# Differential attention: scoring both maps of a head together, the second passes on 64 rows each

## The chip, the core and the metric

The kernel runs on one core of a Trainium2 chip. The metric is the device time of one execution in microseconds (us). The engines are named as the profile names them: PE is TensorE (matrix products), PEld is its weight loads, DVE is VectorE, ACT is ScalarE, POOL is GpSimd, and SP issues most of the transfers.

## The reference, cut to what matters

One layer: a half feed-forward step, a mixer of two attention branches side by side, and a second half feed-forward step. The change lies in branch B of the mixer, differential attention with 4 heads. Each head has two softmax maps over the same 1024 positions; the second, scaled by a learned number, is taken from the first, and the difference multiplies the values:

```
s1 = einsum('bhqd,bhkd->bhqk', qi1, k1) * scale + bias        # d = 64
s2 = einsum('bhqd,bhkd->bhqk', qi2, k2) * scale + bias
p = softmax(where(allowed, s1, NEG)) - lam * softmax(where(allowed, s2, NEG))
out = einsum('bhqk,bhkd->bhqd', p, v)
```

The mask lets a row see whole chunks of 64 up to its own, so a block of 128 query rows, number qb from 0 to 7, needs the first (qb + 1) x 128 keys.

## The kernel before, in words

Products of nearly full float32 accuracy are made from operands in a reduced format (fp32r). Each number x is kept as a high part xH, which is x rounded, and a low part xL, the rest. A product is then xH times yH, plus xL times yH, plus xH times yL, three passes of PE that add up in one bank of PSUM.

In the mixer a *unit* is a pair of stick-breaking heads (units 0 to 3) or one differential head (units 4 to 7). For each unit, QJob and KJob project the queries and the keys. A projection gives 128 rows: 64 for map 0 and 64 for map 1. The depth of a score is only 64, while PE takes 128 rows, and the kernel uses the spare half for the low parts:

- QJob (L1064) writes the tile q. For map i, 64 rows hold qH and the other 64 rows hold qL. For map 0 qH is on the lower half (rows 0 to 63, `lo`), for map 1 on the upper half (`hi`).
- KJob (L1081) writes kd, with kH on both halves, and kl, with kL on both halves. ACT and DVE fill one half, and POOL copies it to the other (L1097 for kd, L1098 for kl).

One score tile z is then two passes of 128 rows, in the function qk (L1164): q against kd (L1169) gives qH kH + qL kH, and q against kl (L1170) adds qH kL and, as a by-product, the tiny qL kL. A z tile is 128 query rows by up to 512 keys (`pieces` cuts the keys at 512); there are three z buffers in PSUM, shared with a few other small tiles.

da_weights (L1269) makes the weights of two query blocks, 2j and 2j + 1. For each block and each map in turn, every piece is scored, DVE subtracts the distance bias from z, writes the result to ex and takes the row maximum (L1280), then DVE negates the maximum (L1286), ACT takes the exponential and the row sum (L1288) and DVE the reciprocal (L1290). At the end of the block DVE scales map 1 (L1295) and subtracts it from map 0 (L1296). The function av transposes these weights (L1188, L1189, tiles trp), and da_out multiplies them by the values (L1306, L1308, tile pav).

Attention alone would leave PE waiting. `fill(n)` therefore puts projection passes of the next unit and of the gates (pps, L1044 to L1048) between the steps of the attention, in proportion. The order on each engine is then fixed when the program is built: a planner takes the recorded instructions and sets each engine's queue, in which instructions run strictly one after the other. Differential units run from about 1041 us to 1340 us of the profile.

Of the kernel before, what the change touches and what calls it, by code (L numbers as in the profile page):

```python
# [12 lines left out]
F32 = mybir.dt.float32  # L13
# [7 lines left out]
P = 128  # L21
D = 1024
S = 1024
NK = D // P
NT = S // P
HALF = 512
# [16 lines left out]
SCALE = 1.0 / math.sqrt(HD)  # L43
# [3 lines left out]
def build(ctx, tc, A, out):  # L47
# [945 lines left out]
    pending = ffn("wg1", "wu1", "wd1", start0, pending0, steps1, lambda c: 0 if c < 3 else 5 if c < 9 else 4 if c == 9 else 0, steps1b, 0, lambda t: A["x"][t * P:(t + 1) * P, :], lambda t: h_dram[0][t])  # L993

    pending = mixer(locals())

    ffn("wg2", "wu2", "wd2", start_half, pending, steps2, lambda c: 2 if c > 1 else 0, no_steps, 2, lambda t: h_dram[1][t],
# [4 lines left out]
def mixer(e):  # L1002
# [5 lines left out]
    V, ACT, PE, POOL, SP = nc.vector, nc.scalar, nc.tensor, nc.gpsimd, nc.sync  # L1008
# [8 lines left out]
    with tc.tile_pool(name="mixa", bufs=1, side="left", reuse_waits="tile") as pa, \  # L1017
            tc.tile_pool(name="mix_ps", bufs=2, space=PSUM, reuse_waits="tile") as psum, stack:
        lo, hi = slice(0, HD), slice(HD, P)


        class Job:


            def __init__(self, srcs):
                self.srcs = srcs
                self.order = (0, 1)
                self.w = None
                self.it = None
# [22 lines left out]
            def columns(self, half):  # L1052

                ps = psum.tile([P, HALF], F32, name="pps", tag="gu")
                H, L = self.w[0]
                yield from self.product(ps, [((H[:, k * P:(k + 1) * P], L[:, k * P:(k + 1) * P]), U[k, half]) for k in range(NK)])
                return ps

            def run(self):
                for half in self.order:  # L1060
                    yield from self.half(half)
                    yield

        class QJob(Job):  # L1064
# [6 lines left out]
            def half(self, half):  # L1071
                if half == 0:
                    self.out = pa.tile([P, 2, S], F32R, name="q", tag="q", bufs=2)
                q = self.out
                sl = slice(half * HALF, (half + 1) * HALF)
                ps = yield from self.columns(half)
                for i, (rh, rl) in enumerate(((lo, hi), (hi, lo))):
                    ACT.mul(q[rh, i, sl], ps[rh], self.scale)
                    V.scalar_tensor_tensor(q[rl, i, sl], ps[rh], self.scale, q[rh, i, sl].bitcast(F32), ALU.mult, ALU.subtract)

        class KJob(Job):  # L1081


            def __init__(self, block):
                super().__init__([A["win"][block]])

            def half(self, half):
                if half == 0:
                    self.out = (pa.tile([P, 2, S], F32R, name="kd", tag="kd", bufs=2),
                                pa.tile([P, 2, S], F32R, name="kl", tag="kl", bufs=2))  # L1090
                kd, kl = self.out
                sl = slice(half * HALF, (half + 1) * HALF)
                ps = yield from self.columns(half)
                for i, (rh, rl) in enumerate(((lo, hi), (hi, lo))):
                    ACT.copy(kd[rh, i, sl], ps[rh])
                    V.tensor_sub(kl[rh, i, sl], ps[rh], kd[rh, i, sl].bitcast(F32))
                    POOL.tensor_copy(kd[rl, i, sl], kd[rh, i, sl])  # L1097
                    POOL.tensor_copy(kl[rl, i, sl], kl[rh, i, sl])  # L1098

        class GateJob(Job):  # L1100
            def __init__(self, gi, c):
# [40 lines left out]
        last_pe = [None]  # L1142
# [3 lines left out]
        def advance(n):  # L1146

            if n > 0 and keep[0]:
                with tc.issue_after(last_pe[0].ins):
                    advance_(n)  # L1150
            else:
                advance_(n)
# [11 lines left out]
        def qk(q, k, i, qb, c0, c1):  # L1164

            z = psum.tile([P, HALF], F32, name="z", tag="z", bufs=3)[:, :c1 - c0]
            qs = slice(qb * P, (qb + 1) * P)
            kd, kl = k
            PE.matmul(z, q[:, i, qs], kd[:, i, c0:c1], start=True, stop=False)  # L1169
            last_pe[0] = PE.matmul(z, q[:, i, qs], kl[:, i, c0:c1], start=False, stop=True)  # L1170
            return z

        def pieces(qb):
            L = (qb + 1) * P
            return L, [(c0, min(c0 + HALF, L)) for c0 in range(0, L, HALF)]
# [59 lines left out]
        def sb_weights(hp, par, j, q, k, fill):  # L1235
            ws = []
            for qb in (2 * j, 2 * j + 1):
                L, cuts = pieces(qb)
                be = mp.tile([P, S], F32, name="be", tag="wa", bufs=4)
                f = mp.tile([P, S], F32, name="f", tag="wb", bufs=2)  # L1240
                for c0, c1 in cuts:
                    z = qk(q, k, par, qb, c0, c1)
                    if c1 == L:
                        PE.matmul(z[:, c1 - P - c0:], identb, mask_sb, start=False, stop=True, skip_group_check=True)
                    ACT.activation(be[:, c0:c1], z, AF.Sigmoid)
                    last_act[0] = ACT.activation(f[:, c0:c1], z, AF.Sigmoid, scale=-1.0)
                    fill(1)
                yield
                fr = f[:, :L][:, ::-1]
                V.tensor_tensor_scan(fr, fr, fr, 1.0, ALU.mult, ALU.bypass)  # L1250
                V.tensor_mul(be[:, :L - 1], be[:, :L - 1], f[:, 1:L])
                ws.append(be)
            yield ws
# [15 lines left out]
        def da_weights(h, j, q, k, fill):  # L1269
            slope = 2.0 ** (-8.0 * (h + 1) / DA_HEADS)  # L1270
            ws = []
            for qb in (2 * j, 2 * j + 1):
                L, cuts = pieces(qb)
                es, rs = [], []
                for m in range(2):
                    ex = mp.tile([P, S], F32, name="ex", tag="wa" if m == 0 else "wb", bufs=4 if m == 0 else 2)
                    mx = mp.tile([P, 2], F32, name="mx", tag="mx", bufs=4)
                    for i, (c0, c1) in enumerate(cuts):
                        z = qk(q, k, m, qb, c0, c1)
                        V.tensor_tensor_reduce(out=ex[:, c0:c1], in0=z, in1=dist[:, S - L + c0:S - L + c1], op0=ALU.subtract,  # L1280
                                               op1=ALU.max, scale=1.0, scalar=NEG, accum_out=mx[:, i:i + 1])
                        fill(1)
                    nm = mp.tile([P, 1], F32, name="nm", tag="nm", bufs=4)
                    if len(cuts) == 2:
                        V.tensor_max(mx[:, 0:1], mx[:, 0:1], mx[:, 1:2])
                    V.tensor_scalar_mul(nm, mx[:, 0:1], -slope)  # L1286
                    sm = mp.tile([P, 1], F32, name="sm", tag="sm", bufs=4)
                    ACT.activation(ex[:, :L], ex[:, :L], AF.Exp, bias=nm, scale=slope, accum_out=sm)  # L1288
                    r = mp.tile([P, 1], F32, name="r", tag="r", bufs=4)
                    V.reciprocal(r, sm)  # L1290
                    es.append(ex)
                    rs.append(r)
                r2 = mp.tile([P, 1], F32, name="r2", tag="r2", bufs=4)
                V.tensor_mul(r2, rs[1], lam)
                V.tensor_scalar_mul(es[1][:, :L], es[1][:, :L], r2)  # L1295
                V.scalar_tensor_tensor(es[0][:, :L], es[0][:, :L], rs[0], es[1][:, :L], ALU.mult, ALU.subtract)  # L1296
                ws.append(es[0])
            return ws
# [30 lines left out]

        def qk_jobs(u):  # L1330
            if u < 4:
                return QJob(u, SCALE), KJob(4 + u)
            h = u - 4
            slope = 2.0 ** (-8.0 * (h + 1) / DA_HEADS)
            return QJob(12 + h, SCALE / slope), KJob(16 + h)


        cur = qk_jobs(0)
        vjob = VJob(0, 0)
        first = [cur[0], cur[1], vjob]  # L1340
# [13 lines left out]
        mp = stack.enter_context(tc.tile_pool(name="mixb", bufs=1, side="right", reuse_waits="tile"))  # L1354
# [13 lines left out]
        for i in range(2):  # L1368
# [7 lines left out]
            ex = mp.tile([P, 1], F32, name=f"le{i}")  # L1376
# [11 lines left out]
        for u in range(8):  # L1388
            sb = u < 4
            if u == 4:  # L1390

                with tc.issue_after(last_act[0].ins):
                    load = ACT.add_instruction(mybir.InstLoadActFuncSet(
                        name=nc.get_next_instruction_name(), engine=ACT.engine, act_func_set_id=EXP_LN_TABLE))
# [3 lines left out]
            if u < 7:  # L1398
                nxt = qk_jobs(u + 1)
                unit_jobs += nxt  # L1400
# [12 lines left out]
            def fill(n):  # L1413
                seen[0] += n * wt[si]
                advance(max(0, min(total, int(total * seen[0] / points)) - done[0]))

            q, k = cur[0].out, cur[1].out
# [62 lines left out]
    with stack0, tc.tile_pool(name="mrg", bufs=1, side="left", reuse_waits="tile") as mp, \  # L1480
# [4 lines left out]
        for half in range(2):  # L1485
            sl = slice(half * HALF, (half + 1) * HALF)
# [14 lines left out]
            for c2 in range(NK // 2):  # L1501
                wb = [split(A[w][c2]) for w in ("wbs", "wbd")]
# [102 lines left out]
```

## Time and profile before

| | |
|---|---|
| Times of three runs | 2197.72, 2198.96, 2202.42 us; median 2198.96 |
| The profiled execution | 2200.5 us, of which the span of its instructions is 2198.7 |
| PE busy | 2136.9 us, 97% of the span |
| DVE, ACT, POOL busy | 1557.2, 1046.9, 60.5 us |
| TensorE clock granted, mean | 0.995 of full speed |
| Scores of differential heads | 96 z tiles: 48 of 512 keys, 16 each of 384, 256 and 128 |

A row of the timeline gives the start in us, the duration in us, the engine, the line of the kernel, the operation, and "written <- read" with the shape. PE's matrix passes overlap: a pass of 512 columns lasts 0.39 us in the record, of which the end is modelled, while the next starts 0.23 us after it. What a pass costs on a busy PE is therefore the distance between starts.

### The profile page before, as it was taken

The numbers are of one execution on the slowest core, as the hardware profiler recorded it, in microseconds if no ns is written. First come the engines' busy times: TensorE is split into PE (matmuls) and PEld (weight loads), VectorE is DVE, ScalarE is ACT, GpSimd is POOL, SyncE is SP. The second block draws the span as 40 slices with busy tenths as digits, with TensorE's granted clock in tenths as the row PEclk, the third lists the DMA queues.
The fourth block names the chain that finished last, engine by engine and source line by source line (L and its number), as shares of the span: only waits on it lengthen the run. The fifth ranks groups of instructions, "written<-read, shape, count | busy, mean of one in ns | idle before, by whom it ended". The sixth has DMA issues, their size and how long they took to land.

```text
span 2198.7 us, 28423 instructions
## 1 busy us (share of the span) xinstructions
PE 2136.9 (97%) x10328; PEld 1772.8 (81%) x10328; DVE 1557.2 (71%) x2629; ACT 1046.9 (48%) x1870; POOL 60.5 (3%) x84
## 2 busy tenths in 40 slices
PE   7999999999999999999999999999999999999997
PEld 5777788878877887987888988888778888888886
DVE  8998876757677678576578576666887767655566
ACT  7532433335456565455445454665733333334453
POOL 0000000000000010101001100000000000000000
PEclk9999999999999999999999999999999999999999
DMA  8588654459784111110212123764476644437675
GB/s 333 171 264 301 214 182 143 156 187 335 250 277 134 41 48 46 33 56 27 70 56 66 44 90 103 240 215 131 136 222 206 225 144 159 158 126 258 199 240 183
DMA packets 139791, 355.50 MB, mean 162 GB/s; under 512 B 19457, under 2 KB 29313, under 8 KB 139650
## 3 DMA queue, kind: packets, MB, share of 16 engines
q1 hardware_dynamic: 138018, 347.91, 47.4%
q0 software_dynamic: 1632, 5.77, 0.7%
q8 instruction: 81, 1.33, 0.3%
q14 instruction: 60, 0.49, 0.1%
HBM read 265.00 MB, written 88.62 MB: 161 GB/s over the span
## 4 chain that ended last, share of the span: by engine, by line
PE 75%; DVE 12%; DMA 8%; ACT 3%; issue 2%; SPq 0%; DVEq 0%; ACTq 0%
PE bank L318 10%; PE bank L320 10%; PE bank L319 10%; PE bankA L630 6%; PE bankB L630 5%; PE pps L1044 5%; PE pps L1046 5%; PE pps L1048 5%; DMA stg<-d_T 2%; DVE f L1250 1%; PE vps L1044 1%; PE vps L1048 1%; PE vps L1046 1%; PE pav L1261 1%; DMA wada<-in_wada 1%
## 5 line engine op out<-in xcount | busy, mean ns | idle before, releaser
L1044 PE MATMUL pps<-uH,wsH 128*128 128x512 f32 x512 | 209.7, 410 | 0.0
L1046 PE MATMUL pps<-uL,wsH 128*128 128x512 f32 x512 | 204.7, 400 | 0.0
L1048 PE MATMUL pps<-uH,wsL 128*128 128x512 f32 x512 | 203.3, 397 | 0.0
L237 DVE TENSOR_TENSOR tbL<-stg,tbH 128x512 fp32r<-128x512 f32 x154 | 106.0, 690 | 100.1 <-ACT tbH L236 99.5
L236 ACT CAST tbH<-stg 128x512 fp32r<-128x512 f32 x154 | 95.6, 621 | 142.5 <-DMA stg<-d_T 105.2
L630 PE MATMUL bankA<-tbL,sbH 128*128 128x512 f32 x352 | 138.4, 393 | 3.9 <-DVE tbL L237 3.8
L319 PE MATMUL bank<-uL,wsH 128*128 128x512 f32 x352 | 138.4, 394 | 3.6 <-DVE uL L819 3.6
L318 PE MATMUL bank<-uH,wsH 128*128 128x512 f32 x352 | 137.9, 397 | 2.1 <-DVE q L401 1.3
L630 PE MATMUL bankA<-tbH,sbH 128*128 128x512 f32 x352 | 135.0, 393 | 3.9 <-ACT tbH L236 1.8
L320 PE MATMUL bank<-uH,wsL 128*128 128x512 f32 x352 | 138.0, 393 | 0.6 <-DVE wsL L237 0.5
L630 PE MATMUL bankA<-tbH,sbL 128*128 128x512 f32 x352 | 137.2, 390 | 1.2 <-DVE sbL L237 1.2
L139 DVE TENSOR_TENSOR wsL<-raw,wsH 128x1024 fp32r<-128x1024 f32 x72 | 88.0, 1222 | 64.2 <-ACT wsH L139 59.6
L237 DVE TENSOR_TENSOR sbL<-stg,sbH 128x512 fp32r<-128x512 f32 (+1 forms) x176 | 108.4, 620 | 23.8 <-ACT sbH L236 23.3
L236 ACT CAST sbH<-stg 128x512 fp32r<-128x512 f32 (+1 forms) x176 | 98.1, 564 | 52.1 <-DMA stg<-hd_A 33.6
L236 ACT CAST wsH<-raw 128x1024 fp32r<-128x1024 f32 (+1 forms) x84 | 69.3, 826 | 99.0 <-PE bank L319 87.1
L1048 PEld LDWEIGHTS pps<-uH,wsL 128*128 128x128 f32 x512 | 96.9, 189 | 17.8
L1044 PEld LDWEIGHTS pps<-uH,wsH 128*128 128x128 f32 x512 | 97.7, 191 | 14.8
L1046 PEld LDWEIGHTS pps<-uL,wsH 128*128 128x128 f32 x512 | 97.3, 190 | 14.2
L139 ACT CAST wsH<-raw 128x1024 fp32r<-128x1024 f32 x72 | 75.4, 1049 | 65.6 <-PE pps L1046 36.5
L630 PE MATMUL bankB<-tbH,sbH 128*128 128x512 f32 x264 | 102.7, 389 | 0.0
L630 PE MATMUL bankB<-tbL,sbH 128*128 128x512 f32 x264 | 102.7, 389 | 0.0
L630 PE MATMUL bankB<-tbH,sbL 128*128 128x512 f32 x264 | 102.7, 389 | 0.0
(259 smaller groups left out, 5816.0 us busy)
## 6 DMA issues: line engine op xcount, KB each, us to landing
wada<-in_wada SPq DMA_DIRECT2D x56, 512.0 KB, 5.6
raw<-in_wg SPq DMA_DIRECT2D x50, 512.0 KB, 6.7
raw<-in_wu SPq DMA_DIRECT2D x50, 512.0 KB, 4.8
raw<-in_wd SPq DMA_DIRECT2D x44, 512.0 KB, 5.2
stg<-d_S SPq DMA_DIRECT2D x88, 256.0 KB, 3.6
stg<-d_T SPq DMA_DIRECT2D x88, 256.0 KB, 3.6
d_S<-s SPq DMA_DIRECT2D x40, 512.0 KB, 5.4
d_T<-t SPq DMA_DIRECT2D x40, 512.0 KB, 5.4
```

The lines of the kernel that those rows point to most:

```text
L139: made[:] = ACT.copy(h, raw).ins, eng.tensor_sub(l, raw, h.bitcast(F32)).ins
L236: ACT.copy(h, src)
L237: eng.tensor_sub(l, src, h.bitcast(F32))
L318: PE.matmul(ps, H[:, ks], bH, start=first and k == 0, stop=False, skip_group_check=not first)
L319: PE.matmul(ps, H[:, ks], bL, start=False, stop=False, skip_group_check=not first)
L320: PE.matmul(ps, L[:, ks], bH, start=False, stop=k == 3, skip_group_check=not first)
L630: PE.matmul(ps, a[:, ts], b, start=first and n == 0, stop=last and n == 2, skip_group_check=not check)
L1044: PE.matmul(ps, aH, bH, start=i == 0, stop=False)
L1046: PE.matmul(ps, aH, bL, start=False, stop=False)
L1048: PE.matmul(ps, aL, bH, start=False, stop=i == n - 1)
L1250: V.tensor_tensor_scan(fr, fr, fr, 1.0, ALU.mult, ALU.bypass)
L1261: PE.matmul(pav[:, qs], vt[:, kb, h % 4].rearrange("p a d -> p (a d)"), w, start=first, stop=last)
```

## The change

Both maps of a head are scored together, in the new function qk2. It takes two z buffers, runs the full first pass of map 0 and of map 1, and then the two second passes. A second pass now uses only the 64 rows that hold qH: the lower half for map 0 and the upper half for map 1. The program gives these passes the shape of a 64-row tile of the array, at row 0 for map 0 and at row 64 for map 1; every other pass keeps the shape of the whole array. The by-product qL kL is no longer computed for these heads.

```diff
-            def __init__(self, block):
+            def __init__(self, block, both):
...
                     POOL.tensor_copy(kd[rl, i, sl], kd[rh, i, sl])
-                    POOL.tensor_copy(kl[rl, i, sl], kl[rh, i, sl])
+                    if self.both:
+                        POOL.tensor_copy(kl[rl, i, sl], kl[rh, i, sl])
...
+        def qk2(q, k, qb, c0, c1):
+
+            zs = [psum.tile([P, HALF], F32, name="z", tag="z", bufs=3)[:, :c1 - c0] for _ in range(2)]
+            qs = slice(qb * P, (qb + 1) * P)
+            kd, kl = k
+            for m, z in enumerate(zs):
+                PE.matmul(z, q[:, m, qs], kd[:, m, c0:c1], start=True, stop=False)
+            for m, z in enumerate(zs):
+                rows = (lo, hi)[m]
+                last_pe[0] = PE.matmul(z, q[rows, m, qs], kl[rows, m, c0:c1], start=False, stop=True)
+            return zs
...
-                es, rs = [], []
-                for m in range(2):
-                    ex = mp.tile([P, S], F32, name="ex", tag="wa" if m == 0 else "wb", bufs=4 if m == 0 else 2)
-                    mx = mp.tile([P, 2], F32, name="mx", tag="mx", bufs=4)
-                    for i, (c0, c1) in enumerate(cuts):
-                        z = qk(q, k, m, qb, c0, c1)
+                exs = [mp.tile([P, S], F32, name="ex", tag="wa" if m == 0 else "wb", bufs=4 if m == 0 else 2) for m in range(2)]
+                mxs = [mp.tile([P, 2], F32, name="mx", tag="mx", bufs=4) for m in range(2)]
+                for i, (c0, c1) in enumerate(cuts):
+                    zs = qk2(q, k, qb, c0, c1)
+                    for z, ex, mx in zip(zs, exs, mxs):
                         V.tensor_tensor_reduce(out=ex[:, c0:c1], in0=z, in1=dist[:, S - L + c0:S - L + c1], op0=ALU.subtract,
                                                op1=ALU.max, scale=1.0, scalar=NEG, accum_out=mx[:, i:i + 1])
                         fill(1)
+                es, rs = exs, []
+                for ex, mx in zip(exs, mxs):
                     nm = mp.tile([P, 1], F32, name="nm", tag="nm", bufs=4)
...
-                return QJob(u, SCALE), KJob(4 + u)
+                return QJob(u, SCALE), KJob(4 + u, True)
...
-            return QJob(12 + h, SCALE / slope), KJob(16 + h)
+            return QJob(12 + h, SCALE / slope), KJob(16 + h, False)
```

The queues of PE, DVE and ACT are planned anew around the differential heads. SP's queue keeps its order, and POOL's loses 16 copies of kl.

PE's queue at the first long block of unit 4 (queries 256 to 383, map 0 in z_10022 and map 1 in z_10047), before:

```order
L1169 MATMUL z_10022<-kd_9026,q_8864 128x384
L1170 MATMUL z_10022<-kl_9027,q_8864 128x384
L1044 MATMUL pps_10034<-uH0_0_5768,wsH_9623 128x512
L1046 MATMUL pps_10034<-uL0_0_5769,wsH_9623 128x512
L1048 MATMUL pps_10034<-uH0_0_5768,wsL_9624 128x512
L1044 MATMUL pps_10034<-uH1_0_5793,wsH_9623 128x512
L1169 MATMUL z_10047<-kd_9026,q_8864 128x384
L1170 MATMUL z_10047<-kl_9027,q_8864 128x384
```

The same place on PE after the change (map 0 in z_10020, map 1 in z_10021; L1181 is the first pass and L1184 the 64-row second pass):

```order
L1181 MATMUL z_10020<-kd_9026,q_8864 128x384
L1181 MATMUL z_10021<-kd_9026,q_8864 128x384
L1184 MATMUL z_10020<-kl_9027,q_8864 128x384
L1184 MATMUL z_10021<-kl_9027,q_8864 128x384
L1044 MATMUL pps_10035<-uH0_0_5768,wsH_9624 128x512
L1046 MATMUL pps_10035<-uL0_0_5769,wsH_9624 128x512
L1048 MATMUL pps_10035<-uH0_0_5768,wsL_9625 128x512
```

The four score passes stand together, and the projection passes that lay between the maps follow in one run of eight instead of two of four. Of the 48 pairs of second passes, 42 stand side by side in PE's queue (23 of 512 keys, 8 of 384, 5 of 256, 6 of 128). In the other 6 (1 of 512, 3 of 256, 2 of 128) something stands between the two. That makes 54 stretches of 64-row passes, each with passes of the whole array before and behind it.

DVE's queue at the next step of that unit (queries 512 to 639, in pieces of 512 and 128 keys), before:

```order
L1280 ISA ex_10154,mx_10155<-z_10156,dist_6503 128x512
...
L1194 TENSOR_TENSOR tL_10151<-trp_10145,tH_10150 128x512
L1323 TENSOR_TENSOR ms_10124<-ms_10124,ln_10136 128x256
L1280 ISA ex_10154,mx_10155<-z_10164,dist_6503 128x128
...
L1324 TENSOR_TENSOR ms_10124<-ms_10124,ln_10136 128x256
L1285 TENSOR_TENSOR mx_10155<-mx_10155 128x1
L1325 TENSOR_SCALAR ms_10124<-ms_10124 128x256
L1286 TENSOR_SCALAR nm_10172<-mx_10155 128x1
L1280 ISA ex_10179,mx_10180<-z_10181,dist_6503 128x512
```

And after (ex_10148 is map 0, ex_10149 is map 1; L1293 is the reduction, L1301 the negated maximum):

```order
L1293 ISA ex_10148,mx_10150<-z_10152,dist_6503 128x512
...
L1337 TENSOR_TENSOR ms_10118<-ms_10118,ln_10130 128x256
L1293 ISA ex_10149,mx_10151<-z_10153,dist_6503 128x512
...
L1338 TENSOR_TENSOR ms_10118<-ms_10118,ln_10130 128x256
L1339 TENSOR_SCALAR ms_10118<-ms_10118 128x256
L1293 ISA ex_10148,mx_10150<-z_10168,dist_6503 128x128
...
L1340 SCALAR_TENSOR_TENSOR ln_10130<-ln_10130,subs_6507,ms_10118 128x256
L1293 ISA ex_10149,mx_10151<-z_10169,dist_6503 128x128
...
L1301 TENSOR_SCALAR nm_10184<-mx_10150 128x1
L1301 TENSOR_SCALAR nm_10191<-mx_10151 128x1
```

The reductions of both maps now alternate, and the negated maximum of map 0, which its exponential waits for, stands behind all four reductions of the block rather than behind its own two.

More of the change, by code (lines that the diff above doesn't have):

```diff
@@ L1081, in mixer @@
         class KJob(Job):
-            def __init__(self, block):
+            def __init__(self, block, both):
                 super().__init__([A["win"][block]])
+                self.both = both
             def half(self, half):
@@ L1290, in da_weights @@
                     V.reciprocal(r, sm)
-                    es.append(ex)
                     rs.append(r)
```

## The prediction

> **What bounds the kernel.** I read the page first: busy shares and the chain that ended last.
>
> ```profile
> span 2198.7 us, 28423 instructions
> PE 2136.9 (97%) x10328; PEld 1772.8 (81%) x10328; DVE 1557.2 (71%) x2629; ACT 1046.9 (48%) x1870; POOL 60.5 (3%) x84
> PE 75%; DVE 12%; DMA 8%; ACT 3%; issue 2%; SPq 0%; DVEq 0%; ACTq 0%
> ```
>
> PE is the bound of the kernel as a whole, but what counts is the stage of the change. So next the busy time by stretches of 25 us through the differential heads (us, then PE, PEld, DVE, ACT, POOL, each with its count, the granted clock, the share of DMA):
>
> ```profile
> 1040.00:1065.00 25.00, 21.59 (x111) 18.62 (x110) 20.16 (x41) 15.49 (x29) 0.00 (x0) 0.86 0.30 87
> 1090.00:1115.00 25.00, 25.00 (x130) 21.14 (x129) 21.28 (x71) 14.17 (x32) 5.60 (x8) 1.00 0.20 72
> 1190.00:1215.00 25.00, 24.65 (x137) 20.67 (x136) 21.85 (x75) 14.41 (x31) 0.00 (x0) 1.00 0.16 53
> 1315.00:1340.00 25.00, 24.84 (x129) 20.71 (x128) 22.48 (x78) 15.17 (x29) 0.00 (x0) 1.00 0.33 106
> ```
>
> After the first stretch PE is full, with DVE behind it at 85 to 90% in the densest stretches. The waits of PE and PEld between 1040 and 1340 us (who waited for whom: us, times, longest) confirm it:
>
> ```profile
> PE trp L1189 <- DVE ex L1296: 0.6, 2, 0.4
> PE z L1169 <- ACT f L1246: 0.5, 1, 0.5
> PEld pn L1317 <- ACT ms L1313: 2.4, 7, 0.5
> PEld trp L1189 <- DVE ex L1296: 1.6, 3, 0.7
> PEld z L1169 <- POOL kl L1098: 0.4, 1, 0.4
> ```
>
> No score pass waited for a z buffer, and finished weights (L1296) held PE up by a microsecond or two in all. So here a PE pass that goes away shortens the kernel by its distance between starts, and a gap on PE lengthens it likewise. What matters is what the passes cost, which the timeline shows:
>
> ```profile
> 1327.38 0.39 PE L1048 MATMUL pps<-uH,wsL 128*128 128x512 f32 x1
> 1327.38 0.19 PEld L1169 LDWEIGHTS z<-kd,q 128*128 128x128 f32 x1
> 1327.61 0.33 PE L1169 MATMUL z<-kd,q 128*128 128x384 f32 x1
> 1327.78 0.34 PE L1170 MATMUL z<-kl,q 128*128 128x384 f32 x1
> 1327.95 0.40 PE L1044 MATMUL pps<-uH,wsH 128*128 128x512 f32 x1
> 1098.37 0.22 PE L1169 MATMUL z<-kd,q 128*128 128x128 f32 x1
> 1098.43 0.27 PE L1170 MATMUL z<-kl,q 128*128 128x128 f32 x1
> 1098.54 0.45 PE L1048 MATMUL pps<-uH,wsL 128*128 128x512 f32 x1
> 1098.83 0.39 PE L1044 MATMUL pps<-uH,wsH 128*128 128x512 f32 x1
> 1103.37 0.28 PE L1169 MATMUL z<-kd,q 128*128 128x256 f32 x1
> 1103.48 0.28 PE L1170 MATMUL z<-kl,q 128*128 128x256 f32 x1
> 1103.60 0.40 PE L1044 MATMUL pps<-uH,wsH 128*128 128x512 f32 x1
> ```
>
> A pass of 512 columns costs 0.23 us (1327.38 to 1327.61), one of 384 costs 0.17, one of 256 costs 0.115. The weights of the next pass load while a pass runs (PEld at 1327.38). The two of 128 show what limits short passes: 0.06 us after the first the second starts, but the pass behind them holds PE for 0.29 us instead of 0.23, so both together cost 0.23, 0.115 each. I read that as the shortest distance between two weight loads.
>
> **The change part by part.** *Second passes side by side.* Both second passes of a pair keep a weight load each, and if they stream together, one pass per pair goes. During the first pass of map 1 (0.227 us for 512 columns; 23 starts from 1119.81 to 1125.03 us) two loads must now fit:
>
> ```profile
> 1119.81 0.39 PE L1170 MATMUL z<-kl,q 128*128 128x512 f32 x1
> 1125.03 0.27 PE L1188 MATMUL trp<-ident,ex 128*128 128x128 f32 x1
> ```
>
> Two loads need 0.23 us by the rows of 128. So a pair of 512 saves its whole 0.227, a pair of 384 saves 0.17 less the 0.06 by which the loads outlast the pass, 0.11, and pairs of 256 and 128 save nothing, being bound by loads already. With the 42 pairs that stand side by side in the queue: 23 x 0.227 + 8 x 0.11 = 6.1 us. Were the loads of the two halves free of each other, it would be 23 x 0.227 + 8 x 0.17 + 5 x 0.115 + 6 x 0.06 = 7.5 us; if the passes don't stream together, 0. I take 6.1, because the rows of 128 show the load limit. The 6 pairs that stand apart save nothing.
>
> The Trainium skill gives a number for the first half of this: in "TensorE: Matmul & The Clock Gate", section "Part 3: Packing small matmuls — row/col tiling", matmuls on different row groups start some 4 ns apart. By it the sum would differ by under 0.2 us; no run here has yet shown such a pair.
>
> *Changing shape.* 54 stretches of 64-row passes make 108 changes between whole array and half array. The trace of before has no such change, so I bound one. From below: a change to another kind of pass, transposes to projections, costs nothing.
>
> ```profile
> 1125.36 0.27 PE L1189 MATMUL trp<-ident,ex 128*128 128x128 f32 x1
> 1125.39 0.48 PE L1046 MATMUL pps<-uL,wsH 128*128 128x512 f32 x1
> 1125.70 0.40 PE L1048 MATMUL pps<-uH,wsL 128*128 128x512 f32 x1
> ```
>
> From the last transpose to L1048 it is 0.34 us, which is 0.11 for the transpose and 0.23 for the pass, with no gap. From above: when PE had to stop, the pass after the stop shows what a load costs that could not be made ahead.
>
> ```profile
> 1038.79 0.19 PEld L1169 LDWEIGHTS z<-kd,q 128*128 128x128 f32 x1 [0.28 <-ACT f L1246]
> 1038.79 0.51 PE L1169 MATMUL z<-kd,q 128*128 128x512 f32 x1
> 1039.13 0.39 PE L1170 MATMUL z<-kl,q 128*128 128x512 f32 x1
> ```
>
> Here 0.34 us pass until the next start instead of 0.23, so the bare load costs 0.11. If the array must also run empty first, the tail of a pass comes on top, 0.39 - 0.23 = 0.16 (a modelled end): 0.27 in all. Between 0 and 0.27 neither row is clearly near. The next weights load ahead here past every other change of kind, which speaks for the low end; a changed shape alters which rows add up to which output, which speaks against 0. I take half a bare load, 0.055, so 108 x 0.055 = 5.9 us.
>
> *Order on DVE and ACT.* The same reductions run, 0.69 us each for 512 columns, but the exponential of map 0 can start only after the last reduction of map 1, so the weights of a block are ready later by about one exponential.
>
> ```profile
> L1280 DVE CUSTOM_DVE_ANT_0 ex<-z,dist 128x512 f32<-128x512 f32 x48 | 32.8, 685 | 4.2 <-PE z L1170 3.5
> L1288 ACT ACTIVATE ex<-ex,nm 128x1024 f32<-128x1024 f32 x8 | 9.2, 1153 | 5.5 <-DVE nm L1286 5.5
> ```
>
> The cover is the filling behind the last pair, which grows by 4 projection passes (0.9 us) because the whole run of eight now comes after it, against an exponential of at most 1.15 us. Where unit 7 fills thinly, and transposes already waited, up to half a microsecond a step may show. Bounds -0.6 (the waits vanish) to +4 us (16 steps of 0.25); I take +0.5.
>
> *Two z buffers at once.* Of three buffers one is free when a pair begins; the other must have been reduced. Between pairs lie eight filling passes, 1.8 us, against two reductions of 0.69; in unit 7 four passes, 0.9 us, plus the pair's own first pass. Cost nothing, hidden by the filling; without this cover PE would wait out a reduction, 0.69 us a pair.
>
> *Copies of kl.* 16 fewer on POOL, 0.68 us each, on an engine that is 3% busy. One score had waited 0.4 us for such a copy (the last row of waits above); that goes: -0.4.
>
> ```profile
> L1098 POOL CAST kl<-kl 64x512 fp32r<-64x512 f32 x12 | 8.2, 682 | 2.6 <-DVE kl L1096 1.8 <-DVE r L1294 0.2 <-DVE mx L1285 0.2
> ```
>
> The sum is -6.1 + 5.9 + 0.5 - 0.4 = -0.1 us. The profiled execution took 2200.5 us (span 2198.7, 1.8 around it), 1.5 above the median of 2198.96; the difference applies to the median: 2199 us.
>
> **The rivals.** *Free changes.* If changing shape costs next to nothing (under 0.02 us), the saving stands: -6.1 + 0.1, 2193 us. The unbroken starts around the transposes speak for it; that no row shows a change of shape leaves it open.
>
> *Each change empties PE's pipeline.* Then a change costs between a bare load and a load with a tail: 108 x 0.11 - 6.1 = +5.8, or 108 x 0.27 - 6.1 = +23, so 2205 to 2222 us, slower. It decides above about 0.10 us per change: 10.5 us lost against 6.1 saved. For it speaks that a stopped PE shows just this price at 1038.79; against it, that loads here run ahead of everything. The Trainium skill, "TensorEngine Tiling (Array Packing)", section "Key Properties", speaks for this rival: changing the tiling mode, not just the tile, drains TensorE. It names no price, and no row here has such a change to weigh it by.
>
> *The passes don't stream together.* The change then does not do what it says: nothing is saved, and only the price of changing shape is left, 2199 us where that is nothing and 2205 where it is half a bare load. Nothing in the trace speaks for or against it.
>
> *Late weights.* If the transposes wait the full 4 us, my sum becomes +3.4, 2202 us; with free changes it would be 2197.
>
> **How the numbers follow.** A measurement of this kernel can tell about 0.2%, 4.4 us, from no change. My forecast, a change price between 0.02 and 0.095 that roughly eats the saving: 0.36. Free changes: 0.26. Pipeline emptied: 0.30. Not streaming together: 0.06, half of it slower. Late weights with the rest as forecast: 0.02, within the bound. So faster 0.26, within 0.36 + 0.02 + 0.03 = 0.41, slower 0.33. The price 0.055 gives 2199 us. The range begins at 2192.5, free changes with a little more than 6.1 saved, and ends at 2213, a change price of 0.185 (108 x 0.185 - 6.1 = +13.9); beyond lie the dearer half of the emptied pipeline, about 0.13, and 0.04 below.
>
> **What would show it.** In the timeline after, the two second passes of a pair start within hundredths of a microsecond of each other, and a group of four 512-column passes spans three times 0.227 up to the following projection, plus twice the price of a change. If that span is over 0.91, the change loses on PE. Waits of score passes on DVE (L1293) would show that the z buffers run short, and more waits of transposes on DVE (L1310) that weights come late. The forecast is wrong if a change of shape costs nothing or more than 0.1.

## The result, and the profile after

The changed kernel takes 2210.86 us (median of 6 runs, 2207.29 to 2213.66), against 2199.22 us (6 runs, 2196.64 to 2202.42) for the kernel before. The ratio is 1.005, with a 95% interval of 1.0037 to 1.0062: half a per cent slower, some 11 us. The profiled execution took 2211.82 us. Its page, in the lines that answer to those of before:

```profile
span 2210.0 us, 28407 instructions
PE 2151.6 (97%) x10328; PEld 1767.0 (80%) x10328; DVE 1554.7 (70%) x2629; ACT 1045.0 (47%) x1870; POOL 49.4 (2%) x68
PE 72%; DVE 12%; DMA 9%; ACT 3%; issue 2%; SPq 0%; DVEq 0%; ACTq 0%
```

The number of passes on PE is the same, and PE is busy 14.7 us longer. The page doesn't tell where. For that, two group rows mark the ends of the stage in each trace: the last mask pass of the stick-breaking units and the first merge pass (L197). The first two rows are of before, the last two of after; each gives its group's shortest, median and longest duration in ns and its first and last start.

```profile
L1244 PE MATMUL z<-mask_sb,identb x64: 219/230/330, 741.4 to 1039.4; 128*128 128x128 bf16 x64
L197 PE MATMUL bps<-uH,wsH x128: 389/389/580, 1364.5 to 1495.8; 128*128 128x512 f32 x128
```
```profile
L1258 PE MATMUL z<-mask_sb,identb x64: 219/230/330, 740.4 to 1040.0; 128*128 128x128 bf16 x64
L197 PE MATMUL bps<-uH,wsH x128: 389/389/577, 1375.2 to 1507.6; 128*128 128x512 f32 x128
```

From the last mask pass to the first merge pass it is 325.1 us before and 335.2 us after: 10.1 us, nearly the whole difference. From there to the end of the last pass it is 823.5 and 824.1 us. The length between the two marks, called the stage below, is used for every experiment, because it leaves out what varies elsewhere: the part ahead of it alone takes 1034.4 to 1040.5 us in the profiles of this document. Each stage is read from one profiled execution, so a few tenths of a microsecond between two stages say nothing. The granted clock doesn't make differences between stages: in each of the nine profiles it falls to 0.5 once, for 6.8 us, some 5 to 6 us into the stage, and is 1.00 in the rest of it.

Inside the stage PE stays full but gets less done (windows after; columns as in the prediction):

```profile
1090.00:1115.00 25.00, 24.98 (x122) 19.24 (x121) 20.62 (x68) 13.19 (x29) 3.13 (x4) 1.00 0.21 68
1190.00:1215.00 25.00, 25.00 (x129) 19.04 (x128) 18.53 (x60) 12.49 (x26) 0.00 (x0) 1.00 0.22 73
1315.00:1340.00 25.00, 25.00 (x119) 17.70 (x117) 22.92 (x87) 13.84 (x31) 0.00 (x0) 1.00 0.15 54
```

PE starts 122, 129 and 119 passes in 25 us where it started 130, 137 and 129, at the same granted clock, and "busy" doesn't show it. The mix of passes in a window moves a little, so this is a hint only. The waits of the weight loads name the place (after, 1040 to 1375 us: us in all, times, longest; the rows for pn and pav, 2.2 and 2.1 us where before has 3.0 and 2.4, are left out):

```profile
PEld z L1184 <- issue: 11.8, 38, 0.4
PEld pps L1044 <- issue: 2.8, 12, 0.2
PEld pps L1048 <- issue: 2.8, 12, 0.2
PEld trp L1203 <- DVE ex L1310: 2.0, 6, 0.8
PEld pps L1046 <- issue: 1.8, 8, 0.2
```

Four of these five rows have no releaser ("issue"): a load of the 64-row passes (L1184), or of the projection behind them, goes late although nothing that the profile knows holds it. The timeline of one group of 512 keys shows how (the first passes of both maps, the two second passes in one row, then projections):

```profile
1103.67 0.40 PE L1181 MATMUL z<-kd,q 128*128 128x512 f32 x1
1103.91 0.40 PE L1181 MATMUL z<-kd,q 128*128 128x512 f32 x1
1104.23 0.19 PEld L1184 LDWEIGHTS z<-kl,q 64*128 64x128 f32 x2 [0.37 <-issue]
1104.23 0.50 PE L1184 MATMUL z<-kl,q 64*128 64x512 f32 x2
1104.66 0.19 PEld L1048 LDWEIGHTS pps<-uH,wsL 128*128 128x128 f32 x1 [0.24 <-issue]
1104.67 0.50 PE L1048 MATMUL pps<-uH,wsL 128*128 128x512 f32 x1
1105.00 0.40 PE L1044 MATMUL pps<-uH,wsH 128*128 128x512 f32 x1
1105.24 0.39 PE L1046 MATMUL pps<-uL,wsH 128*128 128x512 f32 x1
```

Read the starts. The two second passes share a row because they start 4 ns apart (1104.234 and 1104.238): they do run side by side. But the load of a 64-row pass, and that of the pass behind it, starts with its own pass instead of during the pass before. The distances are 0.32 us into the 64-row passes, 0.43 out of them and 0.34 behind the first whole pass, where passes of 512 columns have 0.227 elsewhere. Three distances thus come to 1.09 us instead of 0.68; of the 0.41 too much the change wins back 0.227, the pass that is gone. This group costs 0.18 us more than before. From the first score pass (1103.674) to the projection (1104.666) it is 0.99 us, over the 0.91 that the prediction named as the span from which the change loses on PE.

### The profile page after: what moved, and what is told of

Same layout as the page of the kernel before. It is cut to its first block, busy times and chain, and to the rows that moved or that the text cites. A ratio compares the mean times of both kernels' runs of the same rounds, so it can differ in the third digit from the quotient of the medians.

```text
span 2210.0 us, 28407 instructions
## 1 busy us (share of the span) xinstructions
PE 2151.6 (97%) x10328; PEld 1767.0 (80%) x10328; DVE 1554.7 (70%) x2629; ACT 1045.0 (47%) x1870; POOL 49.4 (2%) x68
## 4 chain that ended last, share of the span: by engine, by line
PE 72%; DVE 12%; DMA 9%; ACT 3%; issue 2%; SPq 0%; DVEq 0%; ACTq 0%
PE bank L320 10%; PE bank L318 10%; PE bank L319 10%; PE bankA L630 6%; PE pps L1044 5%; PE pps L1046 5%; PE pps L1048 5%; PE bankB L630 4%; DMA stg<-d_T 2%; DVE f L1264 1%; PE vps L1044 1%; PE vps L1048 1%; PE vps L1046 1%; PE pav L1275 1%; DMA wada<-in_wada 1%
```

## The experiments

The experiments were timed beside the kernel before, which took 2197.5 us next to the first four of them and 2198.1 next to the last three, so the ratios compare better than the times. The stage of before is 325.1 us.

| | stretches of 64-row passes | stage, us | time, us | ratio to before, 95% interval |
|---|---|---|---|---|
| after | 54 | 335.2 | 2210.9 | 1.005 (1.0037 to 1.0062) |
| order only | 0 | 327.9 | 2201.5 | 1.002 (1.0008 to 1.0031) |
| 64 rows only | 96 | 358.8 | 2234.9 | 1.0165 (1.0149 to 1.0181) |
| second passes twice | 55 | 346.9 | 2222.5 | 1.0113 (1.0096 to 1.013) |
| 64 rows for map 0 alone | 48 | 341.1 | 2213.4 | 1.0074 (1.0059 to 1.0089) |
| order, early exponentials | 0 | 325.5 | 2200.2 | 1.001 (0.9999 to 1.0021) |
| change, early exponentials | 54 | 335.1 | 2210.9 | 1.0053 (1.0037 to 1.0069) |
| both second passes on one half | 54 | 343.8 | 2217.5 | 1.0085 (1.0068 to 1.0102) |

The theory after this trace: PE pays at both edges of a stretch of 64-row passes, whatever lies between. Rivals: the new order pays (late weights, two z buffers at once), or each 64-row pass does.

**Order only.** The changed kernel with second passes on all 128 rows.

```diff
-                rows = (lo, hi)[m]
-                last_pe[0] = PE.matmul(z, q[rows, m, qs], kl[rows, m, c0:c1], start=False, stop=True)
+                last_pe[0] = PE.matmul(z, q[:, m, qs], kl[:, m, c0:c1], start=False, stop=True)
...
-            return QJob(12 + h, SCALE / slope), KJob(16 + h, False)
+            return QJob(12 + h, SCALE / slope), KJob(16 + h, True)
```

> The new order with second passes of all 128 rows (and all copies of kl). If the price lies in changing the shape of the array (0.21 us each way by the trace after), nothing of the loss is left: 2199 us, within 3 us, and no 0.2 us gaps around score passes. If the loss comes from the new order (late exponentials, two z buffers at once), 2210 us.

Most of the loss is gone, so the 64-row passes make it. But 2.8 us of stage stay (4.0 us of time), and the waits point to a reason. Of PEld and PE in this kernel, 1040 to 1375 us:

```profile
PEld trp L1202 <- DVE ex L1309: 4.5, 7, 0.9
PEld z L1181 <- DVE mx L1292: 0.5, 2, 0.3
PE trp L1202 <- DVE ex L1309: 1.9, 5, 0.5
```

Transposes wait longer and more often for finished weights (L1309 is L1296 of before, where the prediction's rows have 1.6 us on PEld and 0.6 on PE). The two scores that wait for a reduction (0.5 us) are the only sign of the z buffers.

**64 rows only.** The kernel before, in its own order, with each second pass on its 64 rows: 96 lone passes, so none runs beside another.

```diff
-        def qk(q, k, i, qb, c0, c1):
+        def qk(q, k, i, qb, c0, c1, rows=slice(0, P)):
...
-            last_pe[0] = PE.matmul(z, q[:, i, qs], kl[:, i, c0:c1], start=False, stop=True)
+            last_pe[0] = PE.matmul(z, q[rows, i, qs], kl[rows, i, c0:c1], start=False, stop=True)
...
-                        z = qk(q, k, m, qb, c0, c1)
+                        z = qk(q, k, m, qb, c0, c1, (lo, hi)[m])
```

> The old order with second passes of 64 rows, one at a time: 96 lone stretches, no two side by side. Price of changing shape: a lone pass costs 0.42 us more at 512 columns, 0.41 at 384, 0.40 at 256, 0.34 at 128, so 48 x 0.42 + 16 x 1.15 = +38.6 us, about 2237 us. If the order is to blame: 2199 us.

The price stands without any change of order: 33.7 us of stage for 96 stretches, 0.35 us each on average, against 38.6 expected. The time is 37.3 us longer than that of the kernel before beside it. A lone pass in the timeline:

```profile
1126.60 0.40 PE L1169 MATMUL z<-kd,q 128*128 128x512 f32 x1
1126.92 0.18 PEld L1170 LDWEIGHTS z<-kl,q 64*128 64x128 f32 x1 [0.36 <-issue]
1126.93 0.50 PE L1170 MATMUL z<-kl,q 64*128 64x512 f32 x1
1127.35 0.50 PE L1044 MATMUL pps<-uH,wsH 128*128 128x512 f32 x1
1127.69 0.40 PE L1046 MATMUL pps<-uL,wsH 128*128 128x512 f32 x1
```

The distances are 0.33, 0.42 and 0.34 us, those of the pair above: one pass or two side by side take PE the same time. In the clear a stretch costs 1.09 - 0.68 = 0.41 us. Stretches of 384 and 256 keys cost 0.40 to 0.41 by their median distances as well; those of 128, which already paid for their loads before, some 0.29.

**Second passes twice.** Behind each pair of second passes the same pair runs once more, which adds that part of the score twice.

```diff
             for m, z in enumerate(zs):
                 rows = (lo, hi)[m]
+                PE.matmul(z, q[rows, m, qs], kl[rows, m, c0:c1], start=False, stop=False)
+            for m, z in enumerate(zs):
+                rows = (lo, hi)[m]
                 last_pe[0] = PE.matmul(z, q[rows, m, qs], kl[rows, m, c0:c1], start=False, stop=True)
```

> The changed kernel with each pair of 64-row second passes issued twice in a row (the small term is added twice, so the scores are not the reference's). If the price is paid once per stretch, a further pair costs only its stream, 24 x 0.227 + 8 x (0.17 + 0.115 + 0.09) = 8.4 us on top of the changed kernel: 2219 us. If every 64-row pass or pair pays it, 48 x 0.4 us more on top: 2238 us. If loads of the two halves follow each other (0.23 us a pair), the short pairs cost 0.23 each: 2222 us.

The stage grows by 11.6 us over after, far from a second price per pair, but also 3.2 us more than the stream alone. The time, 2222.5 us, is that of the third case, loads of the two halves that follow each other. The distances don't bear that case out: by their medians a repeated pair costs 0.23, 0.18, 0.12 and 0.11 us for 512, 384, 256 and 128 keys, not 0.23 for each. Where the two passes of a pair stand apart, each is repeated by itself, so these come to 24 x 0.23 + 8 x 0.18 + 12 x 0.12 + 9 x 0.11 = 9.4 us; the 55th stretch adds some 0.35, and the last 2 us or so are open. The timeline (L1187 is the repeated pair):

```profile
1102.59 0.50 PE L1184 MATMUL z<-kl,q 64*128 64x512 f32 x2
1102.70 0.19 PEld L1187 LDWEIGHTS z<-kl,q 64*128 64x128 f32 x2
1102.93 0.40 PE L1187 MATMUL z<-kl,q 64*128 64x512 f32 x2
1103.26 0.50 PE L1048 MATMUL pps<-uH,wsL 128*128 128x512 f32 x1
1103.60 0.40 PE L1044 MATMUL pps<-uH,wsH 128*128 128x512 f32 x1
```

Between passes of one shape the loads go ahead again (1102.70, beside the pass of 1102.59). So the price hangs on going from passes of one kind to the other and not on the 64-row pass as such. (No kernel ran a pass of 64 rows in the shape of the whole array, so shape and number of rows change together in every run; that it is the shape is not shown apart.) The row also takes the price apart: the first pass of either shape holds PE for 0.34 us (1102.59 to 1102.93, 1103.26 to 1103.60), a pass plus 0.11, which is the bare load of the prediction's row at 1038.79; the last pass before a change holds it for 0.32 to 0.33 us (1102.93 to 1103.26), a pass plus about 0.10. At 512 columns each change costs about 0.10 + 0.11 = 0.21 us.

**64 rows for map 0 alone.** Pairs as in the change, but map 1's second pass on all 128 rows: 48 lone stretches, nothing side by side.

```diff
-                rows = (lo, hi)[m]
+                rows = (lo, slice(0, P))[m]
...
-            return QJob(12 + h, SCALE / slope), KJob(16 + h, False)
+            return QJob(12 + h, SCALE / slope), KJob(16 + h, True)
```

> The new order, the second pass of map 0 on 64 rows, that of map 1 on all 128: 48 lone stretches, nothing side by side. If the two 64-row passes of the changed kernel really save a pass by running together, this is dearer than it: half of the lone price, 38.6 / 2 = 19 us over the kernel before, 2218 us. If running side by side saves nothing, it is no slower than the changed kernel, 2210 us or less.

The stage is 16.0 us longer than before, 0.33 us for each stretch. The time was 4.6 us below the expectation, of which 1.5 lie in the kernel before (2197.5 us here, not 2199); most of the rest is the price per stretch, which was taken in the clear (0.40 on average) where the stage of 64 rows only shows 0.35. It is still above after, by 5.9 us of stage with six stretches fewer: what is missing here are passes that run side by side.

**Order with early exponentials.** To see whether the 2.8 us of the order are late weights, the maximum and the exponential of a map now stand right behind that map's last reduction, ahead of the other map's. Both kernels that follow have this edit; the first has second passes on all 128 rows besides, as order only:

```diff
                     for z, ex, mx in zip(zs, exs, mxs):
                         V.tensor_tensor_reduce(out=ex[:, c0:c1], in0=z, in1=dist[:, S - L + c0:S - L + c1], op0=ALU.subtract,
                                                op1=ALU.max, scale=1.0, scalar=NEG, accum_out=mx[:, i:i + 1])
+                        if i < len(cuts) - 1:
+                            fill(1)
+                            continue
+                        nm = mp.tile([P, 1], F32, name="nm", tag="nm", bufs=4)
+                        ...
+                        ACT.activation(ex[:, :L], ex[:, :L], AF.Exp, bias=nm, scale=slope, accum_out=sm)
                         fill(1)
```

> The order of the change with full 128-row second passes, but each map's maximum and exponential issued right behind that map's own last reduction, ahead of the other map's (the first order-only run had 2201.5 us, a stage 2.8 us longer than before, and waits of transposes for the finished weights of 4.7 us against 1.9 before). Theory, the loss of the order is that the weights come late by an exponential: the waits of the transposes for the weights go back to about 2 us, the stage to about 325.5 us, the time to about 2199 us. Rival, the loss lies elsewhere in the order (two z buffers wanted at once, the projections bunched into runs of eight): the waits fall but the stage stays near 328 us and the time near 2201.5 us.

```profile
PEld trp L1202 <- DVE ex L1311: 2.4, 5, 0.6
PEld z L1181 <- DVE mx L1293: 0.6, 2, 0.3
PEld z L1181 <- POOL kl L1100: 0.4, 1, 0.4
PE trp L1202 <- DVE ex L1311: 0.5, 2, 0.3
```

PE's own waits for the weights go from 1.9 back to 0.5 us, and the stage from 327.9 to 325.5, that of before within 0.4. The time can't be told from before, and hardly from that of order only (ratios of 1.001 and 1.002 with intervals that overlap). So by the stages and the waits, of one profile each, the order lost by late weights, and nothing points to a second cause.

**The change with early exponentials.**

> The full change with the same early exponentials, the 54 stretches of 64-row passes kept. Theory, the change loses on PE at the two edges of each stretch and the late weights are hidden behind that: the stage stays at 335 us within 0.7, the time near 2210 us. Rival, late weights and changes of shape add up: the stage falls by the 2.8 us of the order, to about 332.5 us, the time to about 2208 us.

```profile
PEld z L1184 <- issue: 11.9, 38, 0.4
PEld trp L1203 <- DVE ex L1312: 0.5, 2, 0.4
```

Here the same edit takes the loads' wait for weights from 2.0 to 0.5 us and wins nothing: 335.1 us against 335.2. A reading that fits is that PE, delayed by the changes of shape, mostly finds the weights ready: in the change it waits 0.4 us for them, in order only 1.9.

**Both second passes on one half.** Both run on the upper 64 rows, so that they can't run side by side (map 0's then multiplies qL by kL).

```diff
-                rows = (lo, hi)[m]
+                rows = hi
...
-            return QJob(12 + h, SCALE / slope), KJob(16 + h, False)
+            return QJob(12 + h, SCALE / slope), KJob(16 + h, True)
```

> The full change, but both second passes of a pair on the upper 64 rows, so that they can't run side by side (map 0's then multiplies qL by kL instead of qH by kL, and the copies of kl are made again). The stretches of 64-row passes stay 54. Theory, the two passes of a pair run side by side in the change and the second is wholly free: here it costs its own distance between starts again, 0.227, 0.17, 0.115 and 0.11 us for 512, 384, 256 and 128 keys, so 24 x 0.227 + 8 x 0.17 + 8 x 0.115 + 8 x 0.11 = 8.6 us more than the change, a stage of about 343.9 us and 2219 us. Rival as the prediction had it, that the loads of the two halves are not free of each other: the change saves 6.1 us only, so 2217 us, and a pair of 256 or 128 costs the same here as in the change. Rival that the passes of a pair saved nothing by running side by side: 2211 us, as the change. A further rival: a change from one half to the same half again also empties the array, then a pair costs 0.2 us more still, 2230 us.

```profile
1102.72 0.39 PE L1181 MATMUL z<-kd,q 128*128 128x512 f32 x1
1103.04 0.50 PE L1184 MATMUL z<-kl,q 64*128 64x512 f32 x1
1103.38 0.39 PE L1184 MATMUL z<-kl,q 64*128 64x512 f32 x1
1103.70 0.50 PE L1048 MATMUL pps<-uH,wsL 128*128 128x512 f32 x1
1104.04 0.40 PE L1044 MATMUL pps<-uH,wsH 128*128 128x512 f32 x1
```

The second pass starts 0.34 us after the first, as the repeated pair did above, so one half twice in a row doesn't empty the array. The stage grows by 8.6 us over after, the figure expected for a second pass that is wholly free in the change, though that sum had counted all 48 pairs, so its exactness is partly chance. The time, 2217.5 us, lies nearer to the rival's 2217 than to 2219, but six runs from 2212.0 to 2221.2 us can't tell them apart. The distances can: that rival had pairs of 256 and 128 keys cost the same here as in the change, and by the medians every size costs more, 0.23, 0.18, 0.11 and 0.11 us for 512, 384, 256 and 128 keys. Over the 42 pairs that stand side by side this is 23 x 0.23 + 8 x 0.18 + 5 x 0.11 + 6 x 0.11 = 7.9 us. That is what running side by side saves; the other 0.7 us are open.

## Where the prediction was right and where it was wrong, step by step

The forecast had the two terms that decide, a saving on PE and a price for changes of shape. The time fell within the range, but the single forecast, a draw at 2199 us, was wrong by 12 us, and a change cost twice the 0.1 us that the prediction named as the sign of its being wrong. What happened is the rival "each change empties PE's pipeline", within the 2205 to 2222 us given for it. That the time lies inside the range is partly luck: with the price measured in the clear the prediction's own sum is 108 x 0.21 - 6.1 = +16.6, 2216 us, beyond its end of 2213. Short passes that paid less and pairs that saved more brought it back.

- **Changing shape** is the step that failed, by its size. The prediction bounded a change by 0 and 0.27 us and took half a bare load, 0.055, because loads ran ahead past every other change of kind. Measured in the clear it is 0.21 us, a whole bare load of 0.11 and about 0.10 before it, which reads as the array running empty and is less than the modelled tail of 0.16. Averaged over the stage (64 rows only: 33.7 us over 192 changes) it is 0.175, since the shortest passes pay less and waits elsewhere shrink. The row that should have led was the stop at 1038.79, where a load had not gone ahead. That other kinds of pass follow each other without a gap said nothing on shapes: they all have the same one.
- On the rule that the prediction cited from the Trainium skill, "TensorEngine Tiling (Array Packing)", section "Key Properties", the trace agrees: a change of mode costs 0.21 us, as a drain would, while going from one 64-row tile to the other costs nothing (4 ns).
- **Second passes side by side** held, and saved more than said: 7.9 us instead of 6.1, above the upper bound of 7.5. The limit of 0.115 us between two loads, read from the passes of 128 keys, doesn't hold between the two halves: their loads start 3 ns apart. So pairs of 256 and 128 keys save a pass as well. The rival that the passes don't stream together falls, and the trace agrees with the 4 ns cited from the Trainium skill, "TensorE: Matmul & The Clock Gate", section "Part 3: Packing small matmuls — row/col tiling": 1104.234 and 1104.238.
- **Order on DVE and ACT**: +0.5 taken, -0.6 to +4 as bounds; alone it is +2.8 us, by the wait named, transposes on DVE's finished weights. In the full change it doesn't show: taking it out there leaves the stage as it was (335.1 and 335.2 us). Late weights as a rival fall.
- **Two z buffers at once** cost nothing that shows: 0.5 and 0.6 us of waits in the two kernels of the order alone, none that the profile lists in the change.
- **Copies of kl**: the 0.4 us wait on POOL is gone, as said; it is back in both kernels of the order alone, which make the copies.

The sum again with what was measured: 54 x 0.35 - 7.9 = +11.0 us, against 10.1 of stage. The 0.35 already holds the waits that vanish, and the order adds nothing beside it. Where the last microsecond lies isn't settled, nor are the some 4 us by which the prices in the clear (80 x 0.41 + 16 x 0.29 = 37.4 us) exceed the 33.7 of the 64-row kernel; the waits of PE that shrink there are 1.6 us of it.

The break-even follows from the timeline: a stretch costs 0.41 us and a pair of 512 keys returns 0.23, so by this estimate at least two such pairs must share a stretch to come out even. That takes four z buffers where there are three, and no kernel here has them. None of the kernels run is faster than the one before.

## What to carry to other kernels

A mixed array shape is paid per stretch, not per pass: count how often PE goes from whole passes to packed ones and back (0.41 us for both ways here, for 512 columns), and compare it with what the packed passes in one stretch save. When a change alters something that no row of the profile shows, take the price from the place where the mechanism had already stopped once, rather than half way to zero, and keep in mind that even that was half of the price here (0.11 of 0.21 us). And a cost measured alone can be invisible in the whole: the late weights cost 2.8 us by themselves and nothing behind PE's own delay.

## What the runs showed of the hardware that was not expected

For passes of 256 to 512 columns the cost of a change hangs neither on the direction nor on the size of the pass: 0.09 to 0.10 us more for the last pass of the old shape, 0.11 more for the first of the new one. At 128 columns a stretch costs 0.29 instead of 0.41 us. Weight loads for the two halves of the array run in parallel (starts 3 ns apart), while for whole-array passes of 128 columns two loads had shown a distance of some 0.11. Within one shape, even on the same half, loads go ahead as usual (1102.70 above), so passes on 64 rows are not slower as such.
